# Issuing a small input transfer on the scalar engine's queue ahead of the kernel's opening barrier

## Chip, cores and metric

One core of a Trainium2 chip. The metric is the device time of one execution in microseconds (us), lower is better. The profile's span is some 1.8 us shorter than that time (779.3 against 781.07 in the profiled run of the kernel before).

## The reference

A mixture of softmaxes: for each of 32 x 128 positions, four softmaxes over 4096 entries are weighted by a softmax over four prior logits.

```python
# logits (32, 128, 4, 4096) f32, prior (32, 128, 4) f32
prior_probs = softmax(prior, axis=-1)
mixture = np.sum(prior_probs[..., None] * softmax(logits, axis=-1), axis=2)   # (32, 128, 4096)
```

The logits are 268.4 MB, the output 67.1 MB, and the prior 64 KB.

## The kernel before

The 4096 positions go through in 32 tiles (`u`) of 128 partitions. One tile's logits are 4 heads x 2 MB, loaded on SP's queue into one of two buffers of `ltile`. ACT (the scalar engine) takes the exponentials and their row sums, DVE (the vector engine) the reciprocals and the weighted sums, POOL (the GpSimd engine) the product of reciprocal and prior probability (`coeff`). SP is the sync engine, which here only issues transfers. Issued transfers stand in line in the rings of the DMA engines. The next load into a buffer waits for that buffer's last reader. The outputs go out on ACT's queue, at the end of the kernel on SP's.

```python
def load(u):                      # tile 0 in two halves of 4 MB, most tiles in one of 8 MB
    ...
    for h, to in zip(cuts, cuts[1:]):
        ld = nc.sync.dma_start(out=ltile[:, u % 2, h:to], in_=lg[u // J, u % J, :, h:to, :])
        if u >= 2:
            only(ld, adds[u - 2, 0] if h == 0 else exps[u - 2, to - 1])
    ...
load(0)
nc.scalar.dma_start(out=pr, in_=pv)          # the prior: 16 partitions x 4 KB
load(1)
nc.gpsimd.memset(pn, 0.0)
nc.vector.reduce_max(pmax, pr, axis=AX.X)
nc.vector.tensor_sub(pr, pr, ...)
nc.scalar.activation(pr, pr, AF.Exp)         # in ACT's order ahead of all logits exponentials
nc.vector.reduce_sum(pmax, pr, axis=AX.X)
nc.vector.reciprocal(pmax, pmax)
nc.vector.tensor_mul(pn[0:G]..., pr, pmax...)
...                                          # four 32x32-block transposes into pp
for u in range(U):
    ...                                      # exp -> dsum -> rden (DVE) -> coeff = rden * pp (POOL) -> weighted sums (DVE)
```

A program opens with a block in which POOL fills some constants and all engines then meet in a barrier; only behind it comes the kernel's body. The kernel before already takes the first logits transfer out of the body and puts it ahead of SP's drain (the instruction that ends SP's own part of the block) in that opening block, once the program is finalized. Buffers and constants that the barrier protects are not touched by that transfer.

The softmax here doesn't subtract the row's maximum and nothing guards it: scores larger than these inputs give would overflow.

Of the kernel before, what the change touches and what calls it, by code (L numbers as in the profile page):

```python
# [10 lines left out]
AX = mybir.AxisListType  # L11


def early_first_load(nc):





    blocks = nc.main_func.blocks  # L20
    first = next(
        (b, i)
        for b in blocks[1:]
        for i in b.instructions
        if i.engine == mybir.EngineType.SP and i.opcode == "DMACopy"
    )
    block, ins = first
    assert not ins.sync_info.on_wait
    block.instructions.remove(ins)
    at = next(  # L30
        n
        for n, i in enumerate(blocks[0].instructions)
        if i.engine == mybir.EngineType.SP and i.opcode == "Drain"
    )
    blocks[0].instructions.insert(at, ins)


@with_exitstack
def kernel(
# [4 lines left out]
    out: bass.AP,  # L44
):
    nc = tc.nc
    nc.at_finalize(early_first_load)
    B, S, H, V = logits.shape
    assert prior.shape == (B, S, H)
    assert out.shape == (B, S, V)  # L50
# [83 lines left out]
    with tc.manual_schedule():  # L134
# [16 lines left out]
        for u in range(U):  # L151
# [40 lines left out]
            for h in range(H):  # L192
# [8 lines left out]
                for k in range(g, h + 1):  # L201
                    n = 2 if u == U - 1 and k == H - 1 else 1
# [42 lines left out]
```

## Time and profile before

| | before |
|---|---|
| time, median of 3 runs | 780.81 us (780.80 to 781.06) |
| span of the profiled run | 779.3 us |
| DVE, ACT busy | 67%, 60% |
| DMA engines busy | 9 tenths or more in 39 of 40 slices |
| bytes moved | 335.66 MB, mean 431 GB/s |

Read the DMA row before the engines' shares: no compute engine is near its limit, the transfers are.

### The profile page before, as it was taken

What the parts mean: (1) busy time and instruction counts of PE and PEld (TensorE: products, weight loads), DVE (VectorE), ACT (ScalarE), POOL (GpSimd) and SP (SyncE); (2) the same over time, 40 slices, a digit from 0 to 9 for tenths busy, and PEclk for the clock granted to TensorE, in tenths of its full rate; (3) what the DMA queues carried; (4) which work ended last, traced back from release to release, by engine and by line L of the source; (5) the groups of instructions that cost most, each with busy time, mean ns of one, the idle gap of its engine ahead of it and who ended that gap; (6) DMA issues with size and microseconds to landing.
All of it is one profiled execution on the core that took longest, in us unless ns stands there. A gap on an engine that the chain in (4) does not pass through costs nothing.

```text
span 779.3 us, 654 instructions
## 1 busy us (share of the span) xinstructions
DVE 521.0 (67%) x174; ACT 466.7 (60%) x258; POOL 8.3 (1%) x41
## 2 busy tenths in 40 slices
DVE  4447875558755587555775557855578655689886
ACT  4476555775457755577555675546765567657782
POOL 0000000000000000000000000000000000000000
DMA  9999999999999999999999999999999999999998
GB/s 407 457 417 401 470 407 434 428 461 428 405 467 403 458 420 433 442 443 418 431 454 407 454 408 467 420 415 447 432 442 417 463 399 463 410 427 433 434 429 377
DMA packets 10117, 335.66 MB, mean 431 GB/s; under 512 B 1136, under 2 KB 1136, under 8 KB 1152
## 3 DMA queue, kind: packets, MB, share of 16 engines
q1 hardware_dynamic: 6048, 276.83, 82.3%
q10 hardware_dynamic: 4064, 58.79, 17.6%
q14 instruction: 5, 0.04, 0.0%
HBM read 268.50 MB, written 67.11 MB: 431 GB/s over the span
## 4 chain that ended last, share of the span: by engine, by line
DMA 64%; ACT 27%; DVE 6%; issue 2%; POOL 0%; DVEq 0%; POOLq 0%
DMA ltile<-in_logits_dram 62%; ACT ebuf L159 19%; ACT ltile L159 8%; DVE obuf L177 5%; DMA out_dram<-obuf 2%; DVE ltile L183 1%; POOL coeff L170 0%; DVE rden L168 0%; DVEq L240 0%; POOLq L240 0%; POOLq L170 0%
## 5 line engine op out<-in xcount | busy, mean ns | idle before, releaser
L183 DVE SCALAR_TENSOR_TENSOR obuf<-ebuf,coeff,obuf 128x4096 f32<-128x4096 f32 x90 | 403.6, 4484 | 3.8 <-POOL coeff L170 0.6
L159 ACT ACTIVATE ebuf<-ltile 128x4096 f32<-128x4096 f32 x90 | 322.9, 3589 | 7.4 <-DMA ltile<-in_logits_dram 7.4
L159 ACT ACTIVATE ltile<-ltile 128x4096 f32<-128x4096 f32 x38 | 137.3, 3614 | 280.6 <-DMA ltile<-in_logits_dram 280.6
L168 DVE RECIPROCAL rden<-dsum 128x4 f32<-128x4 f32 (+1 forms) x36 | 6.3, 175 | 227.9 <-ACT ebuf L159 225.1
L177 DVE TENSOR_SCALAR obuf<-ltile,coeff 128x4096 f32<-128x4096 f32 x30 | 70.6, 2353 | 10.2 <-POOL coeff L170 10.2
L183 DVE SCALAR_TENSOR_TENSOR ltile<-ltile,coeff 128x4096 f32<-128x4096 f32 (+1 forms) x7 | 27.0, 3875 | 0.8 <-POOL coeff L170 0.6
L159 ACT ACTIVATION_READ_ACCUMULATOR ebuf<-ltile 128x1 f32 x90 | 16.8, 186 | 0.0
L170 POOL TENSOR_TENSOR coeff<-rden,pp 128x4 f32<-128x4 f32 (+1 forms) x36 | 7.2, 200 | 755.3 <-DVE rden L168 745.4
L159 ACT ACTIVATION_READ_ACCUMULATOR ltile<-ltile 128x1 f32 x38 | 7.1, 186 | 0.0
L139 DVE TENSOR_REDUCE pmax<-pr 16x256 f32<-16x1024 f32 x1 | 1.2, 1208 | 7.8 <-DMA pr<-in_prior_dram 7.8
L141 ACT ACTIVATE pr<-pr 16x1024 f32<-16x1024 f32 x1 | 1.1, 1055 | 7.8 <-DVE pr L140 7.8
L177 DVE TENSOR_SCALAR ltile<-ltile,coeff 128x4096 f32<-128x4096 f32 x2 | 4.7, 2354 | 0.6 <-POOL coeff L170 0.6
L144 DVE TENSOR_TENSOR pn<-pr,pmax 16x1024 f32<-16x1024 f32 x1 | 1.9, 1939 | 0.1
L141 ACT ACT_TABLE_LOAD x1 | 1.3, 1283 | 1.2 <-PEq L229 1.2
L142 DVE TENSOR_REDUCE pmax<-pr 16x256 f32<-16x1024 f32 x1 | 1.2, 1207 | 1.1 <-ACT pr L141 1.1
L149 DVE STREAM_TRANSPOSE pp<-pn 32x256 f32<-32x256 f32 x4 | 1.7, 435 | 0.1
L143 DVE RECIPROCAL pmax<-pmax 16x256 f32<-16x256 f32 x1 | 1.7, 1741 | 0.0
L140 DVE TENSOR_TENSOR pr<-pr,pmax 16x1024 f32<-16x1024 f32 x1 | 1.2, 1211 | 0.0
L138 POOL MEMSET pn<- 32x1024 f32 x1 | 0.9, 941 | 0.3 <-POOLq L229 0.3
L229 POOL MEMSET const-bfloat16-1.0<- 128x1 bf16 x1 | 0.1, 106 | 0.0
L229 POOL MEMSET const-uint8-127<- 128x1 uint8 x1 | 0.1, 106 | 0.0
L229 POOL MEMSET const-float32-0.0<- 128x1 f32 x1 | 0.1, 103 | 0.2 <-issue 0.2
(1 smaller groups left out, 0.1 us busy)
## 6 DMA issues: line engine op xcount, KB each, us to landing
out_dram<-obuf ACTq DMA_DIRECT2D x28, 2048.0 KB, 29.4
ltile<-in_logits_dram SPq DMA_DIRECT2D x7, 4096.0 KB, 26.1
ltile<-in_logits_dram SPq DMA_DIRECT2D x2, 2048.0 KB, 30.9
out_dram<-obuf SPq DMA_DIRECT2D x2, 2048.0 KB, 33.9
out_dram<-ltile SPq DMA_DIRECT2D x1, 2048.0 KB, 17.2
out_dram<-ltile SPq DMA_DIRECT2D x2, 1024.0 KB, 4.8
ltile<-in_logits_dram SPq DMA_DIRECT2D x28, 30.9
pr<-in_prior_dram ACTq DMA_DIRECT2D x1, 64.0 KB, 7.0
```

The lines of the kernel that those rows point to most:

```text
L139: nc.vector.reduce_max(pmax, pr, axis=AX.X)
L140: nc.vector.tensor_sub(pr, pr, pmax.unsqueeze(2).to_broadcast([G, R, H]))
L141: nc.scalar.activation(pr, pr, AF.Exp)
L142: nc.vector.reduce_sum(pmax, pr, axis=AX.X)
L143: nc.vector.reciprocal(pmax, pmax)
L144: nc.vector.tensor_mul(pn[0:G].rearrange("g h r -> g r h"), pr, pmax.unsqueeze(2).to_broadcast([G, R, H]))
L149: nc.vector.transpose(pp[32 * t : 32 * (t + 1)], pq[:, :, :, 32 * t : 32 * (t + 1)])
L159: ex = nc.scalar.activation(es[h], lt[:, h], AF.Exp, accum_out=dsum[:, u, h : h + 1])
L168: rc = nc.vector.reciprocal(rden[:, u, h : h + n], dsum[:, u, h : h + n])
L170: mul = nc.gpsimd.tensor_mul(coeff[:, u, h : h + n], rden[:, u, h : h + n], ppu[:, h : h + n])
L177: st = nc.vector.tensor_scalar(out=acc[:, lo:hi], in0=es[h][:, lo:hi], scalar1=coeff[:, u, h : h + 1], scalar2=None, op0=ALU.mult,)
L183: st = nc.vector.scalar_tensor_tensor(out=acc[:, lo:hi], in0=es[h][:, lo:hi], scalar=coeff[:, u, h : h + 1], in1=acc[:, lo:hi], op0=ALU.mu ...
```

## The change

The intent: the prior's transfer is the other one that needs nothing from the opening block. If ACT issues it ahead of its own drain, as SP does with the first logits, the prior lands earlier and its softmax can start earlier. The helper becomes a loop over two engines; the rest of the kernel is unchanged.

```diff
-def early_first_load(nc):
+def early_transfers(nc):
     blocks = nc.main_func.blocks
-    first = next(
-        (b, i) for b in blocks[1:] for i in b.instructions
-        if i.engine == mybir.EngineType.SP and i.opcode == "DMACopy"
-    )
-    ...                                   # remove it, insert it ahead of SP's Drain
+    def of(block, engine, opcode):
+        return next((i for i in block.instructions
+                     if i.engine == engine and i.opcode == opcode), None)
+
+    for engine in (mybir.EngineType.SP, mybir.EngineType.Activation):
+        body = next(b for b in blocks[1:] if of(b, engine, "DMACopy"))
+        ins = of(body, engine, "DMACopy")
+        assert not ins.sync_info.on_wait
+        body.instructions.remove(ins)
+        drain = of(blocks[0], engine, "Drain")
+        blocks[0].instructions.insert(blocks[0].instructions.index(drain), ins)
...
-    nc.at_finalize(early_first_load)
+    nc.at_finalize(early_transfers)
```

More of the change, by code (lines that the diff above doesn't have):

```diff
@@ L11 @@
 AX = mybir.AxisListType
-def early_first_load(nc):
+def early_transfers(nc):
     blocks = nc.main_func.blocks
-    first = next(
-        (b, i)
-        for b in blocks[1:]
-        for i in b.instructions
-        if i.engine == mybir.EngineType.SP and i.opcode == "DMACopy"
-    )
-    block, ins = first
-    assert not ins.sync_info.on_wait
-    block.instructions.remove(ins)
-    at = next(
-        n
-        for n, i in enumerate(blocks[0].instructions)
-        if i.engine == mybir.EngineType.SP and i.opcode == "Drain"
-    )
-    blocks[0].instructions.insert(at, ins)
+    def of(block, engine, opcode):
+        return next(
+            (i for i in block.instructions if i.engine == engine and i.opcode == opcode), None
+        )
+    for engine in (mybir.EngineType.SP, mybir.EngineType.Activation):
[5 more added lines that the diff above has]
+        blocks[0].instructions.insert(blocks[0].instructions.index(drain), ins)
 @with_exitstack
```

## The prediction

> **What bounds the kernel now.** I read the DMA line of the profile page first, because an already tuned kernel whose two busiest engines stand at 67% and 60% must be waiting for something else.
>
> ```profile
> span 779.3 us, 654 instructions
> DVE 521.0 (67%) x174; ACT 466.7 (60%) x258; POOL 8.3 (1%) x41
> DMA  9999999999999999999999999999999999999998
> DMA packets 10117, 335.66 MB, mean 431 GB/s; under 512 B 1136, under 2 KB 1136, under 8 KB 1152
> ```
>
> All 40 slices of the DMA row but the last are at nine tenths or more: the transfer engines are busy from end to end and the compute engines fit inside. To see whether anything at the opening is lost at all, I cut the span into stretches and compared their rates (columns: the stretch, its length, busy time and count of DVE, ACT and POOL, the granted clock, the DMA share, GB/s).
>
> ```profile
> 0.00:24.00 24.00, 9.04 (x9) 11.26 (x7) 1.15 (x5) 1.00 0.98 404
> 24.00:48.15 24.15, 15.99 (x5) 12.11 (x7) 0.20 (x1) 1.00 1.00 434
> 48.15:96.50 48.35, 31.97 (x10) 30.94 (x19) 0.40 (x2) 1.00 1.00 426
> 193.00:700.00 507.00, 335.48 (x105) 303.39 (x167) 4.22 (x21) 1.00 1.00 434
> 771.00:779.30 8.30, 2.42 (x2) 0.00 (x0) 0.00 (x0) 1.00 0.72 299
> ```
>
> 434 GB/s is what the transfers settle at. 335.66 MB at that rate are 773.4 us. The first 24 us run at 404, which costs 24 x (1 - 404/434) = 1.7 us; the stretch at 426 costs 0.9; the end after 771 us costs 8.3 x (1 - 299/434) = 2.6. Together 778.6 of the 779.3 us. So the whole opening, with everything that is imperfect in it, holds 1.7 us, and in another cut no byte at all moves in the first 1.00 us: over half of it is the time before the first bytes arrive. No change of the opening can win more than that 1.7 us, 0.2% of the span, unless it removes bytes. This one removes none.
>
> Next, the opening in order of time (start, duration, engine, line, what; in brackets the idle time before and what ended it).
>
> ```profile
> 0.00 1.62 SPq L100 DMA_DIRECT2D ltile<-in_logits_dram  x3
> 0.79 0.39 ACTq L136 DMA_DIRECT2D pr<-in_prior_dram  x1
> 1.21 1.28 ACT L141 ACT_TABLE_LOAD   x1 [1.21 <-PEq L229]
> 7.81 1.21 DVE L139 TENSOR_REDUCE pmax<-pr 16x256 f32<-16x1024 f32 x1 [7.81 <-DMA pr<-in_prior_dram]
> 10.29 1.05 ACT L141 ACTIVATE pr<-pr 16x1024 f32<-16x1024 f32 x1 [7.80 <-DVE pr L140]
> 12.66 3.62 ACT L159 ACTIVATE ltile<-ltile 128x4096 f32<-128x4096 f32 x1 [1.31 <-DMA ltile<-in_logits_dram]
> 16.45 1.78 DVE L149 STREAM_TRANSPOSE pp<-pn 32x256 f32<-32x256 f32 x4
> 29.72 0.18 DVE L168 RECIPROCAL rden<-dsum 128x4 f32<-128x4 f32 x1 [11.50 <-ACT ebuf L159]
> 29.98 0.20 POOL L170 TENSOR_TENSOR coeff<-rden,pp 128x4 f32<-128x4 f32 x1 [28.26 <-DVE rden L168]
> ```
>
> The first logits transfer is issued at 0.00, already ahead of the barrier; the prior's transfer at 0.79, behind it, and it lands at 7.81. The reader should see two idle times here. The first logits exponential (12.66) sat 1.31 us after the prior's own exponential was done (10.29 + 1.05 = 11.34) and was let go by the logits transfer, not by the prior. And the prior's table `pp` is finished at 16.45 + 1.78 = 18.23, while its first reader, the POOL product at 29.98, was let go by the reciprocal `rden`, which had waited for the logits' exponentials. The prior branch thus has 29.98 - 18.23 = 11.75 us to spare. The chain of work that ended last agrees: from its start it runs through logits loads and exponentials, and neither `pr` nor `pp` is in it.
>
> ```profile
> 0.72 0.07 issue
> 0.79 21.57 DMA ltile<-in_logits_dram
> 22.36 0.02 issue
> 22.39 7.32 ACT ebuf L159 x4
> ```
>
> Last, the barrier itself, by the instructions of its line (start at the end of each row).
>
> ```profile
> L229 ACTq DRAIN  x1: 8/8/8, 0.1 to 0.1; - x1
> L229 SPq DRAIN  x1: 126/126/126, 0.4 to 0.4; - x1
> L229 SPq EVENT_SEMAPHORE  x1: 17/17/17, 0.7 to 0.7; - x1
> L229 ACTq EVENT_SEMAPHORE  x1: 17/17/17, 0.7 to 0.7; - x1
> ```
>
> ACT's queue is at its drain at 0.1 us and then stands until 0.7; SP's queue, which has a transfer to issue first, drains at 0.4 and also stands until 0.7. So ACT has about 0.6 us in which it does nothing.
>
> **What the skill says.** The Trainium skill, "DMA: Bandwidth & Descriptors", section "Issuing engines are not separate DMA queues", says that transfers from the scalar and the sync engine end up on the same 16 DMA engines and interleave, and that issuing from several engines saves only sequencer time. The trace agrees in the sum: queues q1 and q10 take 82.3% and 17.6% of the 16 engines' time, together 99.9%. The same page, "Queues, rings and completion order", says that each DMA engine takes turns between rows packet by packet; this fits a 64 KB transfer needing 7.0 us to land behind a 4 MB one in the other queue, but no run yet shows the turn-taking itself. The same page, "Where 436 GB/s comes from", gives a fabric ceiling of 435 GB/s; the steady 434 is that ceiling, so the rate cannot be raised by a better order of issues. (It also names about 358 GB/s as the HBM share of a core, which this trace, with one core at work, does not show as a bound.)
>
> **The change, part by part.** It removes one transfer issue from ACT's queue behind the barrier and puts the same issue in front of ACT's drain. SP's early load is treated as before; only the helper is written as a loop over two engines. No byte, wait, buffer or compute instruction is added or removed.
>
> 1. The issue moves from 0.79 us to about 0.1 us, where ACT now drains: some 0.7 us earlier. It took 0.39 us. Landing moves at least as much earlier. If the prior's 64 KB get into the rings beside an almost empty first load, it could land in 2.5 to 6 us from the span's start in place of 7.81 (an estimate, from bytes first arriving between 1.0 and 1.5 us and the 7.0 us of today). I choose 5.
> 2. The prior branch (reduce, subtract, exponential, reduce, reciprocal, product, transposes: 18.23 - 7.81 = 10.4 us) moves with it, so `pp` is ready near 15.5 us in place of 18.2. Its slack grows from 11.75 to about 14.5 us. Worth on the path: 0.
> 3. The ACT table load starts about 0.4 us earlier, as no issue stands ahead of it behind the barrier (1.21 to about 0.8). ACT's first dependent work starts at 10.29. Worth: 0.
> 4. ACT reaches its drain at about 0.1 + 0.4 = 0.5 us, plus up to the 0.13 us that SP's drain took: 0.5 to 0.65 against SP's 0.4 + 0.13 = 0.53 and a release at 0.7. The barrier slips by 0 to 0.2 us. What follows it is the second logits issue at 0.79. By then the first transfer has 4.19 MB in the rings (128 partitions x 2 heads x 4096 x 4 B), 9.7 us at 434 GB/s. A slip of 0.2 us leaves no gap. Cost: 0.
> 5. Bytes: 64 KB at 434 GB/s are 0.15 us. If they move in the first microsecond, in which the DMA engines carry nothing, this time is won for the logits. If they go in beside the first load, nothing is won, since they lie ahead of that load's landing today too (7.81 against 12.6). Worth: 0 to 0.15 us.
>
> Sum: 0 to -0.15 us, less what an earlier first issue could add to the span's length (rival 3). I take -0.1: 780.81 - 0.1 = 780.7 us.
>
> **The rivals.** (1) The prior was the wait at the opening after all, and the 0.7 us go through to the end: 780.1 us. For it: DVE idles 7.81 us for it, the largest wait of the opening on DVE. Against it: the 1.31 and the 11.75 us of slack, and DMA engines that are full anyway. (2) The early prior gets ahead of the first logits load or delays its issue, or the barrier slips, and everything starts later: 781.0 to 781.3 us. For it: ACT would arrive at the barrier as late as SP. Against it: SP still issues first at 0.00, and the rings hold 9.7 us of work. (3) ACT's issue becomes the first counted instruction and the span begins earlier by some tenths, with nothing slower: 781.0 us. ACT's drain at 0.1 makes it at most a tenth or two. (4) A different interleaving of loads and stores sets in later. At 434 GB/s through 507 us there is no room above, and the stores of the loop are issued on events of ACT which do not move; I give it +-0.5 us.
>
> **Range and chances.** The three runs of before lie within 0.26 us, but executions and chips can differ by a few tenths of a per cent. With the gain bounded by 1.7 us above and by a slip of a few tenths below, I take 779.5 to 781.9 us. 2% would be 15.6 us, nine times all that the opening loses; only a slow or broken execution could do that. Faster 0.01, within 2% 0.98, slower 0.01.
>
> **What would show it.** Right: the prior's issue stands near 0.1 us or before, `TENSOR_REDUCE` of `pr` starts 0.7 to 5 us earlier, the table load starts near 0.8; the first logits exponential still starts at 12.5 to 12.8, let go by the logits transfer; the POOL product still starts near 30 let go by `rden`; the rate beyond 24 us is 434 GB/s, and MB are unchanged. Wrong: step 4, if the second logits issue is later than about 1.0 us and the rings run dry; step 5, if the second logits load lands earlier than 22.36 by more than 0.2 us; the whole argument, if the steady rate differs or `pp` turns up in the chain of waits.

## The result, and the profile after

| | before | after |
|---|---|---|
| time, median (range) | 780.97 us (780.80 to 781.06), 6 runs | 781.04 us (780.95 to 781.20), 6 runs |
| span of the profiled run | 779.3 us | 779.2 us |
| bytes | 335.66 MB | 335.66 MB |
| prior's table `pp` ready | 18.23 us | 15.80 us |
| first `coeff` product on POOL | 29.98 us | 29.98 us |

The ratio is 1.0001, 95% interval 0.9988 to 1.0014: the same time. Ratios here are the mean time of one kernel's fast runs over that of the other's of the same rounds, so not quite the ratio of the medians quoted.

The opening of the kernel after in order of time (start, duration, engine, line, what; in brackets the idle time before and its releaser). Line numbers are two lower than before.

```profile
0.13 0.39 ACTq L134 DMA_DIRECT2D pr<-in_prior_dram  x1
0.94 1.28 ACT L139 ACT_TABLE_LOAD   x1 [0.94 <-PEq L227]
5.39 1.21 DVE L137 TENSOR_REDUCE pmax<-pr 16x256 f32<-16x1024 f32 x1 [5.39 <-DMA pr<-in_prior_dram]
7.88 1.05 ACT L139 ACTIVATE pr<-pr 16x1024 f32<-16x1024 f32 x1 [5.66 <-DVE pr L138]
12.67 3.62 ACT L157 ACTIVATE ltile<-ltile 128x4096 f32<-128x4096 f32 x1 [3.73 <-DMA ltile<-in_logits_dram]
14.02 1.78 DVE L147 STREAM_TRANSPOSE pp<-pn 32x256 f32<-32x256 f32 x4
29.72 0.18 DVE L166 RECIPROCAL rden<-dsum 128x4 f32<-128x4 f32 x1 [13.92 <-ACT ebuf L157]
29.98 0.20 POOL L168 TENSOR_TENSOR coeff<-rden,pp 128x4 f32<-128x4 f32 x1 [28.11 <-DVE rden L166]
```

Set the idle times beside those of before. The prior's reduce starts at 5.39 in place of 7.81, and its exponential at 7.88 in place of 10.29: both 2.4 us earlier. ACT then sits idle for 3.73 us in place of 1.31, and the first logits exponential starts at 12.67 in place of 12.66. DVE idles 13.92 us ahead of the first `rden`, in place of 11.50. The 2.4 us have become longer waits for the same logits.

The barrier's own line in the kernel after:

```profile
L227 SPq DRAIN  x1: 126/126/126, 0.4 to 0.4; - x1
L227 ACTq DRAIN  x1: 145/145/145, 0.6 to 0.6; - x1
L227 SPq EVENT_SEMAPHORE  x1: 17/17/17, 0.9 to 0.9; - x1
```

ACT's drain now starts at 0.6 and takes 145 ns, where it started at 0.1 and took 8 ns. It ends at 0.71, later than SP's drain (0.56), and the release has gone from 0.7 to 0.9. The start of the chain of waits gives two more digits: the second logits issue is at 0.94, where it was at 0.79.

```profile
0.88 0.07 issue
0.94 21.42 DMA ltile<-in_logits_dram
22.36 0.02 issue
22.38 7.32 ACT ebuf L157 x4
```

It is issued 0.15 us later and lands at 22.36 as before. The rates of the stretches (columns as in the prediction) have not moved either, if the view is read with care:

```profile
0.00:24.00 24.00, 9.04 (x9) 11.26 (x7) 1.15 (x5) 1.00 0.98 407
193.00:700.00 507.00, 335.53 (x105) 303.40 (x167) 4.21 (x21) 1.00 1.00 434
771.00:779.20 8.20, 2.37 (x2) 0.00 (x0) 0.00 (x0) 1.00 0.72 299
```

This view books the bytes of a DMA packet whole at the packet's start, and packets of the logits here hold up to 64 KB and mostly take 2.4 us. So 407 in place of 404 in the first 24 us (and 431 in place of 434 in the 24 us behind them) is no gain. With each packet's bytes spread over its duration, the trace has 394 GB/s in the first 24 us both before and after.

### The profile page after: what moved, and what is told of

Same layout as the page of the kernel before. It is cut to its first block, busy times and chain, and to the rows that moved or that the text cites. A ratio compares the mean times of both kernels' runs of the same rounds, so it can differ in the third digit from the quotient of the medians.

```text
span 779.2 us, 654 instructions
## 1 busy us (share of the span) xinstructions
DVE 521.0 (67%) x174; ACT 466.7 (60%) x258; POOL 8.3 (1%) x41
## 2 busy tenths in 40 slices
DMA packets 10117, 335.66 MB, mean 431 GB/s; under 512 B 1136, under 2 KB 1136, under 8 KB 1152
## 4 chain that ended last, share of the span: by engine, by line
DMA 64%; ACT 27%; DVE 6%; issue 2%; POOL 0%; DVEq 0%; POOLq 0%
DMA ltile<-in_logits_dram 62%; ACT ebuf L157 19%; ACT ltile L157 8%; DVE obuf L175 5%; DMA out_dram<-obuf 2%; DVE ltile L181 1%; POOL coeff L168 0%; DVE rden L166 0%; DVEq L238 0%; POOLq L238 0%; POOLq L168 0%
```

## The experiments

The theory: the transfers set the time; what counts at the opening is when the logits stream starts and whether it ever runs dry, and the prior's branch counts only once it is late enough to let the stream run dry. The rivals: the prior's start counts by itself; every delay of the opening chain goes through to the end; or nothing at the opening counts at all. Edits are against the kernel after. A difference of a few tenths of a us lies inside the stated 95% intervals (about 1 us either way); where I use one, I say whether the ranges of the runs overlap. Differences to the kernel after use its 781.04 from other rounds; in the rounds of these runs before had 780.96 to 781.04, so this moves none by more than 0.1 us.

**Neither transfer early.**

```diff
-    nc.at_finalize(early_transfers)
```

> Neither transfer is moved ahead of the barrier. Theory (the transfer rate binds; the prior's branch has slack; only the start of the logits stream counts): the first logits issue moves from 0.00 to about 0.75 us behind the barrier, and the whole stream with it, so the time rises by 0.6 to 0.8 us over the kernel before, to about 781.7 us; the pp table is ready near 18 us and nothing waits for it. Rival (the opening is hidden altogether by later slack): unchanged, 781.0 us. Rival (the prior's issue counts as much as the logits'): the same rise, but then the next run must differ.

Measured: 781.71 us (781.69 to 781.79), before 781.04 (780.88 to 781.18) in the same rounds, so 0.67 us slower, with ranges that do not overlap. First logits issue at 0.74. The prior's is at 0.74 too, where it was at 0.79 before: the kernel before is itself the case with only the logits early, so this pair differs in the logits' issue and hardly in the prior's. The first logits exponential:

```profile
13.30 3.62 ACT L156 ACTIVATE ltile<-ltile 128x4096 f32<-128x4096 f32 x1 [3.73 <-DMA ltile<-in_logits_dram]
```

It starts 0.64 us later than before, and the shift is carried to the end almost whole. The starts of the first exponential of a tile, read from ACT's timelines:

| tile | before | after | neither early | only the prior early | no prior at all |
|---|---|---|---|---|---|
| 0 | 12.66 | 12.67 | 13.30 | 12.95 | 12.16 |
| 1 | 41.73 | 41.73 | 42.38 | 42.08 | 41.21 |
| 2 | 64.58 | 64.45 | 65.19 | 65.41 | 64.61 |
| 10 | 258.16 | 258.09 | 258.78 | 258.92 | 258.05 |
| 21 | 524.29 | 524.24 | 524.92 | 525.09 | 524.24 |

So the opening is not hidden: a later start of the logits stream costs nearly its full amount (0.74 us of issue, 0.67 us of time), which refutes the rival that nothing there counts.

**Only the prior early.**

```diff
-    for engine in (mybir.EngineType.SP, mybir.EngineType.Activation):
+    for engine in (mybir.EngineType.Activation,):
```

> Only the prior's transfer is ahead of the barrier, the first logits transfer behind it. Theory: same time as with neither early, or 0.1 us less, about 781.7 us. The prior meets empty rings and lands far sooner than 5.4 us, near 2 us (1.5 to 3), and pp is ready near 12.5 us, and still nothing is gained. Rival (the prior's start counts): 781.0 us or less.

Measured: 781.81 us (781.66 to 782.18), as slow as with neither early, though the prior lands and starts its softmax earlier than in any other run that transfers it:

```profile
2.20 1.21 DVE L137 TENSOR_REDUCE pmax<-pr 16x256 f32<-16x1024 f32 x1 [2.20 <-DMA pr<-in_prior_dram]
12.95 3.62 ACT L157 ACTIVATE ltile<-ltile 128x4096 f32<-128x4096 f32 x1 [7.21 <-DMA ltile<-in_logits_dram]
```

The prior's reduce starts 3.83 us earlier than with neither early (6.03), ACT idles 7.21 us for the logits, and no time is won. The run has one flaw: ACT's early issue holds the barrier here too, so the logits are issued at 0.94 in place of 0.74, and a gain of up to 0.2 us could hide behind that. The pair of before and after, in which the first logits issue stays at 0.00, has no such flaw and shows no gain either. Together they separate the two early issues: the logits' is worth 0.7 us, the prior's nothing that can be seen.

**No prior transfer at all** (wrong result).

```diff
-        nc.scalar.dma_start(out=pr, in_=pv)
+        nc.gpsimd.memset(pr, 0.5)
```

(with the helper's loop over SP alone)

> Wrong result on purpose: the prior is not transferred at all, a memset of pr on POOL (0.5 everywhere) stands in. Theory: 64 KB less at 434 GB/s are 0.15 us, so 780.8 to 781.0 us; this is the most that any placing of the prior's transfer can win. Rival (the prior's transfer holds up the opening): 0.7 us or more faster, 780.3 us or less.

Measured: 780.95 us (780.89 to 781.09), inside the range of before (780.88 to 781.18) and of the kernel after (780.95 to 781.20). So even the ideal placing of the prior wins nothing that these runs resolve. One thing was not expected: the first logits exponential starts at 12.16, 0.5 us earlier, three times what 64 KB take at 434 GB/s. The table above shows that this is gone at tile 2 (64.61 against 64.58), and at tiles 10 and 21 only 0.11 and 0.05 us are left. The run with only the prior early has the same pattern: against neither early its first exponential starts 0.35 us earlier, though its logits are issued 0.20 us later, and at tile 2 it is 0.22 us later. The packets of the trace show where it is given back: with every DMA engine busy, the kernel after loses 0.5 us against 434 GB/s between 47 and 52 us, and the run without the prior 0.4 us there and 0.6 us more between 60 and 64 us. Why 64 KB hold up the first landings by 0.5 us, and what slows those stretches, these runs do not settle.

**The prior between the halves of the first logits load**, on SP's queue.

```diff
-    for engine in (mybir.EngineType.SP, mybir.EngineType.Activation):
+    for engine in (mybir.EngineType.SP,):
...
             for k in range(h, to):
                 loads[u, k] = ld
+            if (u, h) == (0, 0):
+                nc.sync.dma_start(out=pr, in_=pv)
...
-        nc.scalar.dma_start(out=pr, in_=pv)
```

> The prior goes out on SP's queue between the two halves of the first logits load, so it lands with the first half near 13 us. Theory: the prior's exponential, in order on ACT, holds the first logits exponential until about 16.5 us in place of 12.7; ACT makes part of this up in its 2.4 us wait for the second half, the first coeff comes near 31.5 to 32 in place of 30.0 and the third load is issued near 34.3 in place of 32.6, while the rings hold the second load until about 41.7: the chain of the opening is 1.5 to 2 us later and the time is unchanged, 780.9 to 781.1 us. Rival (a later first coeff goes to the end one to one): 782.5 to 783 us.

Measured: 780.89 us (780.79 to 781.23), before 781.00 in the same rounds. The prior's reduce starts at 12.99, and the prior is now in the chain of waits from 0.79 to 12.96. The first logits exponential starts at 16.44 in place of 12.67. Still:

```profile
31.22 0.20 POOL L169 TENSOR_TENSOR coeff<-rden,pp 128x4 f32<-128x4 f32 x1 [29.50 <-DVE rden L167]
33.84 30.60 DMA ltile<-in_logits_dram
```

The first `coeff` comes at 31.22 and the third load is issued at 33.84, both 1.24 us later than in the kernel after; that load lands at 64.43, the kernel after's at 64.42. It stood in line behind the second load, which lands only just before 41.89, where that tile's first exponential starts. A chain of waits that is 1.24 us longer costs nothing while transfers are queued: the clearest evidence against the rival that each delay goes through. (I had expected 31.5 to 32 and 34.3; ACT made up more than I allowed.)

**The prior behind both halves of the first load.**

```diff
-    for engine in (mybir.EngineType.SP, mybir.EngineType.Activation):
+    for engine in (mybir.EngineType.SP,):
...
-        nc.scalar.dma_start(out=pr, in_=pv)
+        nc.sync.dma_start(out=pr, in_=pv)
```

> The prior goes out on SP's queue behind the two halves of the first logits load; only the first logits transfer is ahead of the barrier. Theory: it lands at about 22 us if the queue is strictly in order of both halves. ACT's queue is in order, so the prior's exponential then stands ahead of the first logits exponential and ACT starts those near 26 us in place of 12.7; the first coeff near 41 us in place of 30, the third load issued near 44 in place of 32.6, against rings that are empty at 41.7 to 42: 2 to 4 us lost, 783 to 785 us. Rival (every us of delay of the first coeff goes to the end): +11 us, 792 us. Rival (hidden whatever): 781.0 us.

Measured: 785.59 us (785.50 to 785.64), 4.6 us slower than the kernel after. The prior's reduce starts at 22.66, the first logits exponential at 26.11, the first `coeff` at 40.88, the third load is issued at 43.50. The rate across that moment, and the issue:

```profile
41.40:44.40 3.00, 2.96 (x2) 2.52 (x1) 0.00 (x0) 1.00 0.00 0
43.50 0.33 SPq L98 DMA_DIRECT2D ltile<-in_logits_dram  x1
```

By the packets of the trace the DMA engines stand idle from 41.36 to 44.45, 3.1 us: the stream has run dry, and this is lost for good. The first 64 KB packets behind the gap then take about 3.2 us, where they took 2.4 ahead of it; this makes up part of the rest of the 4.6 us. The size was 0.6 us above my expectation. I had counted from the landing of the second load to the issue of the third, and left out that about 1 us passes from an issue to its first bytes (43.50 to 44.45), here as at the kernel's start (0.00 to 1.02).

**The prior behind the first two loads.**

```diff
-        nc.scalar.dma_start(out=pr, in_=pv)
         load(1)
+        nc.sync.dma_start(out=pr, in_=pv)
```

(with the helper's loop over SP alone, as above)

> The prior goes out on SP's queue behind the first two whole logits loads, so it lands near 42 us, far beyond its slack. Theory: ACT's first logits exponential starts near 45.5 us behind the prior's, the first coeff near 60, the third load is issued near 63 us with the rings empty since 42: about 21 us lost for good, 802 us (798 to 806). Rival (the ring of later work makes it up): 781 to 785 us.

Measured: 804.71 us (804.68 to 804.83), 23.7 us slower than the kernel after. The prior's reduce starts at 41.77 and the third load is issued at 62.61.

```profile
41.20:63.50 22.30, 12.46 (x12) 19.05 (x11) 0.20 (x1) 1.00 0.00 0
```

22.3 us without a transfer (22.5 by the packets, 41.05 to 63.57), and 23.7 us lost. The placings of the prior (with the logits issued early) thus give a curve with a knee: its reduce at 5.39, 7.81 and 12.99 us costs nothing, at 22.66 4.6 us, at 41.77 23.7 us. The change moved the prior from one point of the flat part to another.

**The barrier held back**, with the kernel after's early issues.

```diff
+    engine = mybir.EngineType.Pool
+    body = next(b for b in blocks[1:] if of(b, engine, "Memset"))
+    for _ in range(SLIP):                     # SLIP = 2, or 4
+        ...                                   # move one memset of the body ahead of POOL's Drain
...
+        for t in (obuf[:, 0], obuf[:, 1], ebuf1, ebuf3)[:SLIP]:
+            nc.gpsimd.memset(t, 0.0)
         load(0)
```

With two memsets:

> The kernel after, with two memsets of a 128x4096 tile on POOL ahead of POOL's drain, to hold the opening barrier. From the 0.94 us of a 1024 wide memset each should take about 3.7 us: the barrier is released near 8.3 us. Theory: the first logits transfer keeps the rings fed until about 11 us, so the second logits issue near 8.4 us comes in time: 781.0 us, no change. Rival (a slip of the barrier goes to the end): 788.4 us.

With four:

> As the run with two, with four memsets: the barrier is released near 15.7 us, past the end of the first logits transfer near 11 to 12.7 us. Theory: the rings run dry for 4 to 6 us and this is lost for good: 785 to 787 us. Rival (a slip goes to the end): 796 us. Rival (it never counts): 781 us.

Measured: 780.98 us (780.85 to 781.04) with two, 785.67 us (785.55 to 786.06) with four, before 780.96 in the same rounds. The barrier is released at 7.56 and 14.48, somewhat earlier than expected. The chain of waits with two memsets, then with four:

```profile
7.63 15.00 DMA ltile<-in_logits_dram
22.63 0.02 issue
```

```profile
14.54 11.99 DMA ltile<-in_logits_dram
26.53 0.02 issue
```

With two, the second logits issue is at 7.63, 6.7 us later than in the kernel after, and it lands at 22.63, 0.27 later, with no time lost. With four it is at 14.54, the DMA engines stand idle from 12.17 to 15.49 (3.3 us, by the packets), and the load lands 4.2 us later, with ACT again waiting for it (1.23 us); the time is 4.6 us longer by the medians (5.0 in the profiled run, its slowest). So the 0.15 us by which the change itself delayed that issue lies far inside what the first transfer's queued bytes cover.

**The last store in four pieces.** This one looks for what is left, as the prediction puts more loss at the end than at the opening.

```diff
-                    n = 2 if u == U - 1 and k == H - 1 else 1
+                    n = 4 if u == U - 1 and k == H - 1 else 1
```

> The kernel after with the very last weighted add and its store cut in four pieces in place of two. By the accounting of the prediction, 2.6 us of transfer time are lost after 771 us against 1.7 at the opening, and the last store is 1 MB that lands 4.8 us after its issue. Theory: with 0.5 MB it lands about 1.2 us earlier, less 0.1 for two more instructions: 779.9 to 780.1 us. Rival (fixed completion time, not bytes, makes the tail): 780.9 us or more.

Measured: 781.36 us (781.32 to 781.66), against 780.96 (780.78 to 781.10) of before: 0.4 us slower, ranges apart. The expectation missed, and the time is the rival's. The rates of the last microseconds, first the kernel after, then this one:

```profile
776.00:777.00 1.00, 0.00 (x0) 0.00 (x0) 0.00 (x0) 1.00 0.95 393
777.00:778.00 1.00, 0.00 (x0) 0.00 (x0) 0.00 (x0) 1.00 0.16 66
```

```profile
776.00:777.00 1.00, 0.00 (x0) 0.00 (x0) 0.00 (x0) 1.00 0.99 406
777.00:778.00 1.00, 0.00 (x0) 0.00 (x0) 0.00 (x0) 1.00 0.29 115
```

When the last store is issued (773.39 and, behind four adds in place of two, 773.70) the DMA engines are still busy with what was queued before; with its own bytes they stay so until 777 in both, and the last packet ends at 777.96 and 778.10. A smaller last piece does not empty them sooner. Most of the 2.6 us that I had booked after 771 us is therefore the 2 us with few or no bytes from 777 to the end, which cutting the store does not touch. What the time behind the last packet consists of, these runs do not show. No version beat both kernels.

## Why the prediction was right

The forecast was 780.7 us in 779.5 to 781.9, with no change over 2%; measured 781.04.

- **The bound.** Right. The transfers run at 434 GB/s in both traces, and the runs in which they run dry for 3.1, 3.3 and 22.5 us lose 4.6, 4.6 and 23.7 us. The cap on any change of the opening holds, since the largest effect of an early issue, that of the logits, is 0.7 us, but its size of 1.7 us was off: it rests on the 404 GB/s of the view that books packets at their start. With the bytes spread over the packets' durations (394 GB/s) the first 24 us lose 2.2 us.
- **Step 1, the landing.** Issue at 0.13 us (about 0.1 forecast), reduce at 5.39 (5 chosen). The 5 was a choice within 2.5 to 6, so the closeness is partly luck.
- **Step 2, the branch.** `pp` ready at 15.80 (15.5 forecast), slack 29.98 - 15.80 = 14.2 us (14.5 forecast), worth nothing. The runs that place the prior elsewhere show the same for a reduce anywhere from 5.39 to 12.99.
- **Step 3, the table load.** It starts at 0.94, where I had about 0.8: the barrier's own slip takes part of the gain back. Worth nothing either way.
- **Step 4, the barrier.** Release from 0.72 to 0.88, within the 0 to 0.2 us stated, with ACT's drain now last (it ends at 0.71, SP's at 0.56). That what SP had queued covers it was shown with a slip forty times as large (6.7 us).
- **Step 5, the bytes.** 0 to 0.15 us. In the trace the later tiles start 0.05 to 0.13 us earlier than before; the median time is 0.07 us higher; the ranges of the runs overlap. A tenth of a us can't be resolved here, and my -0.1 us is neither confirmed nor refuted. The run without the prior bounds it: nothing to be seen there either.
- **Rivals.** The first (0.7 us go through) fell with the run that has only the prior early. The second (the barrier's slip costs 0.2 to 0.5 us) fell with the two memsets. The third did not occur: SP's issue is still the first instruction of the span. The fourth (another interleaving later, up to 0.5 us) did not show: the tiles in the table are never more than 0.13 us apart between before and after. By the number alone these could not be told from the forecast: 781.04 is nearer to the 781.0 of the second and third than to 780.7, and before's own median rose from 780.81 (3 runs) to 780.97 (6 runs). The trace and the experiments decide, not the time.

What in the prediction's account was too coarse: the 2.6 us after 771 us, which I read as a loss next to the opening's. The run with four pieces shows that the engines are busy until 777. One reading was wrong, without consequence: the 7.81 us that DVE waits for the prior are not its largest wait of the opening. That is the 11.50 us ahead of `rden`, a wait for the logits.

## What to carry to other kernels

Two transfers can be moved ahead of the opening barrier by the same trick and be worth quite different things: the one that starts the stream that sets the time is worth nearly its full shift (0.67 of 0.74 us here), the one that feeds a side branch with slack is worth nothing. Before moving an issue, find the first reader of what it loads and look at what released that reader; if it was something else, compute the slack and expect longer idle time in place of a shorter run. And when transfers are the bound, ask of each delay whether the queue ran empty, not whether the chain of waits grew. Read rates over short windows with care: where packets last 2.4 us, a window that shows no bytes need not be idle.

## What the Trainium skill lacked or had wrong

- "DMA: Bandwidth & Descriptors", section "Where 436 GB/s comes from": it says that for transfers between HBM and SBUF the HBM side, about 358 GB/s, binds. With one core at work, loads and stores mixed, the transfers here ran at 434 GB/s through a stretch of 507 us; the fabric's figure is the one that fits. The sentence lacks the condition that other places of the skill give: the same page's measured figures, which it calls single-core numbers, go up to 425 GB/s.
- The same page, "Queues, rings and completion order", says that each engine takes turns between queues by packet, without a figure for what a small transfer then waits. Here 64 KB landed 2.0 us after the issue with nothing ahead of it, 5.2 and 5.3 us when issued within 0.13 us of a 4 MB load on the other queue, and 7.0 us when issued 0.79 us after it.
- "VectorE: DVE Perf Modes", section "The DRAIN you can't avoid", tells of drains outside the kernel's own work, on all engines, as a constant of some 12 ns. If the drains of the opening block here are of that kind, which the page does not settle, they were not constant: POOL's took 191 ns in before and after, ACT's 8 ns with no transfer issue ahead of it and 145 ns with one, SP's 7 ns without (the run with only the prior early) and 126 ns with. With ACT's issue there, the barrier was released 0.16 us later. No page that I read says what an issue ahead of a barrier costs the barrier.
